# Gathers of the routing in a ring of eight rows, one gather per gate step, and splits and one-hots of the gate steps shared out anew

## The chip, the cores and the metric

The kernel runs on one core of one Trainium2 chip. The metric is the device time of one execution in microseconds (us), as the median of several runs. Engines: PE is TensorE's matmuls and PEld its weight loads, DVE is VectorE, ACT is ScalarE, POOL is GpSimd, SP is SyncE, which only issues DMAs here.

## The reference, cut to what matters

One residual block on 512 tokens of width 1024: a mixing layer (gated MLP and attention), then a layer of retrieved experts (PEER). The change lies in the second one:

```
q   = (xb @ w_query)                                   # 8 heads, two halves of 128
sc  = einsum('thpd,hpkd->thpk', q, sub_keys)           # 128 keys per half
s_top, i_top = top_k(sc, 16)
cand     = s_top[..., 0, :, None] + s_top[..., 1, None, :]
cand_idx = i_top[..., 0, :, None] * 128 + i_top[..., 1, None, :]
best, pos = top_k(cand, 16);  eidx = cand_idx at pos;  g = softmax(best)
h   = gelu(einsum('thkd,td->thk', expert_u[eidx], xb))
out = einsum('thk,thkd->td', g * h, expert_v[eidx])    # 16384 experts of width 1024
```

All is float32; the large matmuls are done as three float32r products of a high and a low part (hi, lo).

## The kernel before, in words

The 512 tokens are four tiles of 128. For tile 0 the experts are gathered row by row (128 gathers of u and 128 of v). For the other three tiles (384 tokens) every expert is multiplied densely: the first product gives expert_u times x for 128 blocks of 128 experts, Gelu follows, the result is multiplied by a gate matrix that is zero where an expert wasn't chosen, and the second product sums expert_v. Of the last tile, the last 64 tokens (UX) are an exception: their dot products with u are gathered early (two heads share a row block of 128 partitions, so there are 64 early gathers, HS), and the dense first product covers 320 columns only (NDU).

The stages after the mixing layer, in order of time:

1. The routing, a loop over heads h = 0 to 8. `candidates(h)` loads and splits a part of wq, multiplies, copies scores to SBUF (qt, scr) and takes the best keys on VectorE; `choose` works on the head before. Splits (`load_split`: DMA to raw, hi on ScalarE, lo on VectorE or GpSimd) are on GpSimd here. Two tiles of the first product go with each head, and 8 more (BRIDGE) stand in the last iteration. `indices_early` and `ready_early` put the indices of the early tokens together, `gather_early` gathers rows of u, `dots_early` multiplies them with xbu (in PSUM) and sums. The instructions of this stage are ordered by a scheduler with a cost model; a ring of four rows (ROWE) holds the gathered rows.
2. The gate steps, 48 of them (8 tokens each), in an order written out by hand for TensorE, VectorE, ScalarE and GpSimd (`manual_schedule`). A step makes two one-hot matrices: bm (compare on VectorE, times the gate on GpSimd) and am (compare on VectorE, or eight Abs and a Relu on ScalarE). Two steps later (LEAD) TensorE multiplies them (`products`), ScalarE copies the result to gst, and every second step a store of 1 MB goes to gd in DRAM. In between stand the rest of the early gathers and dots, and tiles of the first product: `here` says how many tiles are done by step n; the last six (LAST) come after the loop. For each tile of tokens `indices_of` and `gates_of` prepare indices and gates; those of the last tile need the early dots (`weights_early`).
3. The last stage, a loop over 64 chunks of two expert blocks. Every fourth chunk loads a group of gates (gc, 1.5 MB). `second_product` splits v, multiplies the activations (act) by the gates, splits them (wh, wl) and multiplies; the first product of the chunk 23 further on (AHEAD) follows. `route_gathered` does the routing of tile 0, two heads at a time, at every fourth chunk (ROUTE) from 0 to 12, and `gather_some` paces its gathers. Only TensorE's order is written out here.

Each engine works through its queue in order. The lines of the profile: L119 and L120 are hi and lo of a split, L484 the dot, L475 the early gather, L491 and L495 the index copies, L566 and L567 the positions in `pairs`, L689 to L692 the indices, L714 and L716 bm, L727, L728 and L730 am, L738 the gate products, L741 the copy to gst, L135 to L137 the first products, L901 to L905 the second, L884 to L891 act, wh and wl, L530 the Gelu.

## Time and profile before

| | |
|---|---|
| median of three runs | 1519.49 us (1512.56 to 1523.55) |
| the profiled execution's own time | 1515.91 us |
| span from its first to its last instruction | 1514.2 us |
| TensorE busy, mean granted clock | 1414.0 us (93%), 0.977 |
| VectorE, ScalarE, GpSimd busy | 1161.0 (77%), 631.6 (42%), 709.4 us (47%) |
| moved by DMA | 396.78 MB, mean 262 GB/s |

A matmul counts as busy from start to modelled end, so a busy TensorE at a lower granted clock does less. The shares are means over stages that differ: the mixing layer until about 240 us, the routing until 440, the gate steps until 644, then the last stage.

### The profile page before, as it was taken

What the parts mean: (1) busy time and instruction counts of PE and PEld (TensorE: products, weight loads), DVE (VectorE), ACT (ScalarE), POOL (GpSimd) and SP (SyncE); (2) the same over time, 40 slices, a digit from 0 to 9 for tenths busy, and PEclk for the clock granted to TensorE, in tenths of its full rate; (3) what the DMA queues carried; (4) which work ended last, traced back from release to release, by engine and by line L of the source; (5) the groups of instructions that cost most, each with busy time, mean ns of one, the idle gap of its engine ahead of it and who ended that gap; (6) DMA issues with size and microseconds to landing.
All of it is one profiled execution on the core that took longest, in us unless ns stands there. A gap on an engine that the chain in (4) does not pass through costs nothing.

```text
span 1514.2 us, 21710 instructions
## 1 busy us (share of the span) xinstructions
PE 1414.0 (93%) x7801; PEld 1243.9 (82%) x7801; DVE 1161.0 (77%) x2360; ACT 631.6 (42%) x1040; POOL 709.4 (47%) x465
## 2 busy tenths in 40 slices
PE   7999999989977876979999999999999999999998
PEld 6886678978977866878988888989898989888877
DVE  5437454879957769948898988887888888788883
ACT  5457543333336655533343433433433433333331
POOL 0000025566649997822445554555555554444530
PEclk9999999999989988989999999999999999999999
DMA  5352235366439998876888999999999999878892
GB/s 182 110 181 70 86 130 161 126 206 205 133 96 309 329 320 256 238 266 237 295 321 294 323 347 352 372 329 334 364 365 353 372 360 364 316 271 326 329 351 102
DMA packets 161100, 396.78 MB, mean 262 GB/s; under 512 B 11792, under 2 KB 74272, under 8 KB 158944
## 3 DMA queue, kind: packets, MB, share of 16 engines
q1 hardware_dynamic: 63696, 200.30, 37.3%
q0 software_dynamic: 46464, 168.61, 30.6%
q10 hardware_dynamic: 50832, 26.48, 6.1%
q8 instruction: 61, 1.00, 0.3%
q14 instruction: 47, 0.39, 0.1%
HBM read 363.86 MB, written 31.46 MB: 261 GB/s over the span
## 4 chain that ended last, share of the span: by engine, by line
PE 47%; DVE 20%; DMA 14%; issue 10%; POOL 7%; ACT 2%; SPq 0%; DVEq 0%; POOLq 0%; ACTq 0%
PE pu L135 6%; PE pu L137 6%; PE pu L136 6%; DMA row<-in_vd,eint 5%; PE pa L901 4%; PE pa L902 4%; PE pa L905 4%; DMA row<-in_ud,eint 3%; DMA rowe<-in_ud,eui 3%; PE pa L135 2%; PE pa L137 2%; PE pa L136 2%; DMA gc<-gd 2%; PE px L902 2%; PE px L905 2%
## 5 line engine op out<-in xcount | busy, mean ns | idle before, releaser
L119 ACT ACTIVATE hi<-raw 128x1024 fp32r<-128x1024 f32 x300 | 317.6, 1060 | 574.4 <-DMA raw<-in_vd 247.0
L120 DVE TENSOR_TENSOR lo<-raw,hi 128x1024 fp32r<-128x1024 f32 x240 | 292.5, 1220 | 85.0 <-ACT hi L119 84.0
L849 POOL DMA_INDIRECT row<-in_vd,eint x128 | 194.6, 1521 | 183.4 <-DVE acc L851 156.7
L838 POOL DMA_INDIRECT row<-in_ud,eint x128 | 188.6, 1474 | 187.5 <-DVE row L840 143.5
L137 PE MATMUL pu<-xch,lo 128*128 128x320 f32 x816 | 253.2, 310 | 12.1 <-POOL lo L120 7.7
L135 PE MATMUL pu<-xch,hi 128*128 128x320 f32 x816 | 254.9, 312 | 6.8 <-ACT act L530 6.8
L136 PE MATMUL pu<-xcl,hi 128*128 128x320 f32 x816 | 252.4, 309 | 0.0
L901 PE MATMUL pa<-hi,wh 128*128 128x512 f32 x512 | 200.6, 392 | 0.0
L902 PE MATMUL pa<-lo,wh 128*128 128x512 f32 x512 | 200.1, 391 | 0.0
L851 DVE SCALAR_TENSOR_TENSOR acc<-row,hw,acc 128x1024 f32<-128x1024 f32 x128 | 165.5, 1293 | 43.4 <-DMA row<-in_vd,eint 43.3
L120 POOL TENSOR_TENSOR lo<-raw,hi 128x1024 fp32r<-128x1024 f32 x60 | 144.3, 2413 | 98.1 <-ACT hi L119 97.6
L840 DVE SCALAR_TENSOR_TENSOR row<-row,xb 128x1024 f32<-128x1024 f32 x128 | 156.0, 1220 | 34.2 <-DMA row<-in_ud,eint 34.1
L137 PEld LDWEIGHTS pu<-xch,lo 128*128 128x128 f32 x816 | 154.3, 189 | 15.4 <-POOL lo L120 9.3
L135 PEld LDWEIGHTS pu<-xch,hi 128*128 128x128 f32 x816 | 154.6, 189 | 9.9 <-ACT act L530 8.3
L905 PE MATMUL pa<-hi,wl 128*128 128x512 f32 x512 | 157.7, 389 | 0.0
L136 PEld LDWEIGHTS pu<-xcl,hi 128*128 128x128 f32 x816 | 154.3, 189 | 1.6
L738 PE MATMUL pa<-bm,am 128*128 128x128 f32 x768 | 109.0, 302 | 35.9 <-POOL bm L716 32.1
L738 PEld LDWEIGHTS pa<-bm,am 128*128 128x128 f32 x768 | 101.6, 213 | 42.4 <-POOL bm L716 38.9
L901 PEld LDWEIGHTS pa<-hi,wh 128*128 128x128 f32 x512 | 96.7, 189 | 20.6
L902 PEld LDWEIGHTS pa<-lo,wh 128*128 128x128 f32 x512 | 96.6, 189 | 20.4
L905 PEld LDWEIGHTS pa<-hi,wl 128*128 128x128 f32 x512 | 96.3, 188 | 20.6
L902 PE MATMUL px<-lo,wh 128*128 128x512 f32 x256 | 101.6, 397 | 6.5 <-DVE lo L120 6.5
(212 smaller groups left out, 2612.6 us busy)
## 6 DMA issues: line engine op xcount, KB each, us to landing
raw<-in_uT SPq DMA_DIRECT2D x128, 512.0 KB, 6.1
raw<-in_vd SPq DMA_DIRECT2D x128, 512.0 KB, 5.8
gd<-gst ACTq DMA_DIRECT2D x24, 1024.0 KB, 6.7
gc<-gd SPq DMA_DIRECT2D x16, 1536.0 KB, 9.9
raw<-in_w_in SPq DMA_DIRECT2D x20, 512.0 KB, 4.6
raw<-in_wq SPq DMA_DIRECT2D x16, 512.0 KB, 3.7
raw<-in_w_out SPq DMA_DIRECT2D x8, 512.0 KB, 4.2
bt<-in_bias SPq DMA_DIRECT2D x8, 256.0 KB, 7.5
```

Of the source, the lines that this page charges most:

```text
L119: nc.scalar.activation(hi, raw, AF.Copy)
L120: eng.tensor_tensor(lo, raw, hi.bitcast(F32), op=ALU.subtract)
L135: nc.tensor.matmul(ps, lh[0], rh[0], start=first, stop=False)
L136: nc.tensor.matmul(ps, lh[0], rh[1], start=False, stop=False)
L137: nc.tensor.matmul(ps, lh[1], rh[0], start=False, stop=last)
L738: nc.tensor.matmul(ps[:, i * P:(i + 1) * P], am[:, 4 * q + i, :], bm[:, 4 * q + i, :], start=True, stop=True)
L838: nc.gpsimd.indirect_dma_start(out=row, out_offset=None, in_=ud, in_offset=bass.IndirectOffsetOnAxis(ap=eint[:, j:j + 1], axis=0))
L849: nc.gpsimd.indirect_dma_start(out=row, out_offset=None, in_=vd, in_offset=bass.IndirectOffsetOnAxis(ap=eint[:, j:j + 1], axis=0))
L851: nc.vector.scalar_tensor_tensor(acc0, row, hw[:, j:j + 1], acc0, op0=ALU.mult, op1=ALU.add)
L901: nc.tensor.matmul(accs[t][half], wh[:, b, tok], w[b][0][:, ds_], start=first, stop=False)
L902: nc.tensor.matmul(accs[t][half], wh[:, b, tok], w[b][1][:, ds_], start=False, stop=False)
L905: nc.tensor.matmul(accs[t][half], wl[:, b, tok], w[b][0][:, ds_], start=False, stop=last)
```

## The change

Early gathers: six instead of three are issued in each routing iteration, from a ring of eight rows (ROWA) in the routing's own pool rq; their dots follow one iteration later, and all that were issued are finished before that pool closes. The 28 that remain go one per step, in steps 0 to 27, with a ring of four in the gate steps' pool gp; dots follow three steps later (LAGE). The early weights are formed at steps 33 and 35, and the gates of the last tile are made a second time at step 39, for its last 64 tokens.

Copies: the index copies of the early tokens, the positions in `pairs` (for `route_gathered` too) and the casts of `indices_of` go from VectorE to ScalarE.

Gate steps: the last two of eight columns of each first one-hot are made on ScalarE, six on VectorE. Two tiles of the first product come at step 0, the other twelve are spread over all steps. Splits alternate between GpSimd and VectorE, and after the loop all are on VectorE. The first chunk's v is loaded and split before the last two tiles.

Last stage: xb0, acc0, the first sc and the first gc are loaded by GpSimd's queue; each later gc is loaded a group ahead. `route_gathered` comes at chunks 0, 6, 12 and 18.

```diff
+ROWA = 8
-LAGE = 2
+LAGE = 3
-SLOW = 20
-EARLY = 3
+EARLY = 6
-SOON = 25
+ON_ACT = 2
-ROUTE = 4
+ROUTE = 6
...
-        row = gat.tile([P, D], F32, name="rowe", tag="rowe", bufs=ROWE)
+        routing = ExitStack()
+        rq = routing.enter_context(tc.tile_pool(name="rq", bufs=1))
+        row = rq.tile([P, D], F32, name="rowe", tag="rowe", bufs=ROWA)
...
-        def gather_early(n):
-
-            rows = []
+        def gather_early(n, rows_of, n_rows):
+
             for j in early[:n]:
-                row = gat.tile([P, D], F32, name="rowe", tag="rowe", bufs=ROWE)
+                row = rows_of.tile([P, D], F32, name="rowe", tag="rowe", bufs=n_rows)
...
-                rows.append((j, row))
+                issued.append((j, row))
             del early[:n]
-            issued.append(rows)
...
-            nc.vector.tensor_copy(eu[P - UX:P, js], eidx[P - UX:P, TT - 1, h * TOPK:(h + 1) * TOPK])
+            nc.scalar.copy(eu[P - UX:P, js], eidx[P - UX:P, TT - 1, h * TOPK:(h + 1) * TOPK])
...
-            nc.vector.tensor_copy(eui[:, js], eu[:, js])
+            nc.scalar.copy(eui[:, js], eu[:, js])
...
-            nc.vector.tensor_scalar(top[:, 1, :, 0, :], pos[:, :, 0, :], float(NK), None, op0=ALU.mult)
-            nc.vector.tensor_copy(top[:, 1, :, 1, :], pos[:, :, 1, :])
+            nc.scalar.activation(top[:, 1, :, 0, :], pos[:, :, 0, :], AF.Copy, scale=float(NK))
+            nc.scalar.copy(top[:, 1, :, 1, :], pos[:, :, 1, :])
...
-            dots_early(1)
-            gather_early(EARLY)
+            dots_early(0)
+            gather_early(EARLY, rq, ROWA)
...
         ready_early(NH - 2)
+        dots_early(0)
         routing.close()
...
-            nc.vector.tensor_copy(ei, eidx[:, t, :])
+            nc.scalar.copy(ei, eidx[:, t, :])
...
-            nc.vector.tensor_copy(ff, ii)
+            nc.scalar.copy(ff, ii)
...
-        def first_one_hot(g, c, on_act):
+        def first_one_hot(g, c):
             it, ni, gt = g
-            ts_ = slice(c * TC, (c + 1) * TC)
-            full = [P, TC, P]
+            ts_ = slice(c * TC, (c + 1) * TC - ON_ACT)
+            full = [P, TC - ON_ACT, P]
             am = gp.tile([P, TC, P], F32, name="am", tag="am", bufs=LEAD + 1)
...
+            nc.vector.tensor_tensor(am[:, 0:TC - ON_ACT, :], iota_k[:, None, :].to_broadcast(full),
+                                    it[:, 0, ts_, None].to_broadcast(full), op=ALU.is_equal)
+
+            for i in range(TC - ON_ACT, TC):
+                nc.scalar.activation(am[:, i, :], iota_k, AF.Abs, bias=ni[:, c * TC + i:c * TC + i + 1])
+            rest = am[:, TC - ON_ACT:, :]
+            nc.scalar.activation(rest, rest, AF.Relu, scale=-1.0, bias=1.0)
             return am
...
+        def rows_of_v(c):
+
+            return [load_split(vd.rearrange("(a b) d -> a b d", b=NB)[:, c * BC + b, :]) for b in range(BC)]
+
...
-        def split_next():
+        def split_next(eng=nc.gpsimd):
             nonlocal split
             if split < AHEAD * BC:
-                split_tile(split, nc.gpsimd)
+                split_tile(split, eng)
                 split += 1
...
+        own = steps - UX // TC
...
-                    ams[n] = first_one_hot(gs[t], c, n % 2 == 1 and n < SOON)
+                    ams[n] = first_one_hot(gs[t], c)
+                if n < own - 7:
+                    gather_early(1, gp, ROWE)
                 dots_early(LAGE)
-                if n < steps:
-                    gather_early((len(early) + max(0, SOON - n) - 1) // max(1, SOON - n))
...
+                if n == own - 7:
+                    assert not early
+                    dots_early(0)
+                    weights_early(0)
+                if n == own - 5:
+                    weights_early(1)
+                if n == own - 1:
+
+                    gs[t] = gates_of(GT + t, ff.pop(t))
+                here = LEAD + (AHEAD * BC - i0 - LAST * BC - LEAD) * (n + 1) // steps
                 while split - len(ready) - i0 < min(here, AHEAD * BC - i0 - LAST * BC):
                     multiply_tile()
-                    split_next()
+                    split_next(nc.vector if split % 2 else nc.gpsimd)
             while ready:
+                if split == AHEAD * BC and not weights:
+                    weights[0] = rows_of_v(0)
                 multiply_tile()
-                split_next()
+                split_next(nc.vector)
...
-        nc.sync.dma_start(xb0, xbd[0])
+        nc.gpsimd.dma_start(xb0, xbd[0])
...
-        nc.sync.dma_start(acc0, x2d[0])
+        nc.gpsimd.dma_start(acc0, x2d[0])
...
+        def load_gates(q, eng):
+            gcs[q] = ep.tile([P, NG, GB, TG], F32, name="gc", tag="gc", bufs=2)
+            eng.dma_start(gcs[q].rearrange("p n b t -> p (n b t)"), gd[q].rearrange("p n f -> p (n f)"))
+
         def second_product(c):
-            if (c * BC) % GB == 0:
...
+            w = weights.pop(c) if c in weights else rows_of_v(c)
+            if c == 0:
+                load_gates(0, nc.gpsimd)
+            gc = gcs[c * BC // GB]
...
+            if c == 1:
+                with tc.issue_after(loads[-1]):
+                    load_gates(1, nc.sync)
+            elif c * BC % GB == 0 and 0 < c * BC < NB - GB:
+                load_gates(c * BC // GB + 1, nc.sync)
```

## Rows read from the trace of the kernel before

**Rows 1.** Busy time by stretch: length, PE, PEld, DVE, ACT, POOL (instructions), PE clock, DMA share, GB/s.

```profile
310.00:440.00 130.00, 116.44 (x668) 107.58 (x666) 113.03 (x488) 40.68 (x69) 77.89 (x44) 0.95 0.50 162
...
644.00:680.00 36.00, 27.70 (x145) 24.81 (x144) 15.56 (x25) 12.97 (x19) 9.58 (x4) 0.86 0.74 264
...
800.00:900.00 100.00, 93.88 (x489) 82.66 (x488) 88.48 (x163) 35.97 (x51) 52.38 (x37) 0.97 0.89 325
900.00:1300.00 400.00, 399.42 (x2204) 361.31 (x2204) 342.00 (x436) 153.88 (x218) 213.89 (x144) 1.00 0.96 356
...
450.00:580.00 130.00, 100.43 (x668) 96.64 (x667) 95.01 (x127) 77.65 (x165) 117.54 (x81) 0.89 0.96 319
```

**Rows 2.** Order of time on GpSimd, one gate step: start, duration, instruction, idle before.

```profile
473.22 1.90 POOL L716 TENSOR_TENSOR bm<-bm,gt 128x1024 f32<-128x1024 f32 x1
475.27 0.98 POOL L475 DMA_INDIRECT rowe<-in_ud,eui  x1 [0.16 <-issue]
...
477.52 2.39 POOL L120 TENSOR_TENSOR lo<-raw,hi 128x1024 fp32r<-128x1024 f32 x1
479.86 1.90 POOL L716 TENSOR_TENSOR bm<-bm,gt 128x1024 f32<-128x1024 f32 x1
```

**Rows 3.** Order of time on TensorE: a late gate step, then four tiles' first and last matmul.

```profile
637.45 2.05 PE L738 MATMUL pa<-bm,am 128*128 128x128 f32 x16 [0.21 <-POOL bm L716]
...
643.83 0.39 PE L135 MATMUL pu<-xch,hi 128*128 128x320 f32 x1
...
657.86 0.31 PE L137 MATMUL pu<-xch,lo 128*128 128x320 f32 x1
```

**Rows 4.** Groups of instructions on VectorE, 240 to 432 us: busy, mean ns, idle before.

```profile
L484 DVE SCALAR_TENSOR_TENSOR rowe<-rowe,px 128x1024 f32<-128x1024 f32 x12 | 14.5, 1213 | 7.9 <-DMA rowe<-in_ud,eui 7.8
L495 DVE CAST eui<-eu 128x16 int32<-128x16 f32 x4 | 11.1, 2779 | 2.0 <-DMA eu<-eidx 2.0
L491 DVE COPY eu<-eidx 64x16 f32<-64x16 f32 x4 | 8.8, 2206 | 0.1
...
L566 DVE TENSOR_SCALAR top<-pos 128x48 f32<-128x48 uint32 x8 | 6.0, 752 | 0.0
```

**Rows 5.** Order of time on VectorE, a step with one gather, and the next.

```profile
579.83 1.22 DVE L714 TENSOR_TENSOR bm<-iota_k,pa 128x1024 f32<-128x1024 f32 x1
...
583.24 1.22 DVE L714 TENSOR_TENSOR bm<-iota_k,pa 128x1024 f32<-128x1024 f32 x1
```

**Rows 6.** Groups of instructions on ScalarE, 440 to 645 us.

```profile
L741 ACT COPY gst<-pa 128x512 f32<-128x512 f32 x96 | 55.3, 585 | 78.0 <-PE pa L738 69.9 <-DMA gd<-gst 7.9
L727 ACT ACTIVATE am<-iota_k,ni 128x128 f32<-128x128 f32 x96 | 29.3, 389 | 1.8 <-ACT gst L741 1.8
...
L728 ACT ACTIVATE am<-am 128x1024 f32<-128x1024 f32 x12 | 12.7, 1058 | 0.4
```

**Rows 7.** DMA issues of the page: queue, count, KB each, us to landing.

```profile
raw<-in_uT SPq DMA_DIRECT2D x128, 512.0 KB, 6.1
...
gd<-gst ACTq DMA_DIRECT2D x24, 1024.0 KB, 6.7
```

**Rows 8.** Order of time on VectorE, where the gate steps begin.

```profile
439.58 0.23 DVE L689 CAST ei<-eidx 128x128 int32<-128x128 f32 x1 [10.81 <-PE pu L137]
...
441.79 1.22 DVE L714 TENSOR_TENSOR bm<-iota_k,pa 128x1024 f32<-128x1024 f32 x1 [1.26 <-ACT ni L705]
```

**Rows 9.** Order of time on VectorE, the second norm.

```profile
210.55 1.28 DVE L156 SCALAR_TENSOR_TENSOR xs<-x,rstd,g2row 128x1024 f32<-128x1024 f32 x1
...
219.11 3.21 DVE L156 SCALAR_TENSOR_TENSOR xs<-x,rstd,g2row 128x1024 f32<-128x1024 f32 x1
```

**Rows 10.** Waits of TensorE, 240 to 440 us: total, times, longest.

```profile
PE pu L135 <- ACT act L530: 7.6, 1, 7.6
```

**Rows 11.** Order of time on TensorE, after the gate steps.

```profile
663.61 0.64 PE L135 MATMUL pu<-xch,hi 128*128 128x320 f32 x1 [5.44 <-ACT act L530]
...
669.33 0.80 PE L902 MATMUL px<-lo,wh 128*128 128x512 f32 x1 [2.86 <-DVE lo L120]
```

**Rows 12.** Waits from 640 us to the end.

```profile
DVE act L884 <- DMA gc<-gd: 30.3, 8, 16.2
```

41 lines of the change are left out of this document (10 added, 31 removed).

## The prediction

> **What bounds the kernel now.** I read the busy time by stage first [rows 1]. From 900 to 1300 us TensorE is busy 399.42 of 400 us at full clock: the last stage, from about 680 us on, runs at TensorE's own rate, so whatever lets it start earlier moves the end by as much. Before it there are losses. From 450 to 580 us, in the gate steps, TensorE is busy 100.43 of 130 us at a granted clock of 0.89, while GpSimd is busy 117.54 and the DMA engines 0.96 of the time. From 644 to 680 us, where the last stage begins, TensorE has 27.70 of 36 us at 0.86. From 310 to 440 us, in the routing, VectorE has 113.03 of 130 and TensorE 116.44.
>
> Then GpSimd's order of time in the gate steps [rows 2]. One step with a tile to split goes from 473.22 to 479.86, 6.64 us: the product bm 1.90, two gathers of about 0.96 with 0.3 us between them, the split lo 2.39, and the next product at once. GpSimd waits for nobody there, so it sets the pace, with the DMA engines close behind. TensorE needs far less in a step: 16 matmuls for the gates take 2.05 us [rows 3]. Four tiles of the first product took 643.83 to about 658.0, so 3.5 us a tile [rows 3].
>
> Now the 14 tiles of the loop all fall into the first 18 steps (20 tiles over 25 steps, stopped at 14), on top of up to two gathers a step. Later steps have neither, and TensorE just follows at 2.05 us with 0.21 us of waiting.
>
> **The gate steps.** The early gathers are 64. Before, the routing had done 12 of the dot products [rows 4] and 52 were left for the gate steps. After, six are issued in each of iterations 3 to 8 of the routing loop (16 new ones come in at 3, 5 and 7, so six are always there): 36 in the routing, 28 left, one per step in steps 0 to 27. The tiles are spread: two at step 0, 12 over 48 steps, a quarter of a tile per step. Half of those splits go to VectorE. Two of eight columns of each first one-hot go to ScalarE, where before every second one-hot of steps 1 to 23 did so whole.
>
> The nearest rows to a step after the change are in this trace: from 579.83 to 583.24 VectorE does both one-hots whole and one dot product, 3.41 us, with one gather on GpSimd [rows 5]. The parts of a step with a gather, after:
> VectorE: bm and dot 1.14 each (the 3.41 is three operations of one length), am three quarters of it, 0.85, an eighth of a split at 1.14 = 0.14: 3.27 us.
> GpSimd: 1.90 + 0.98 + 0.16 between them + an eighth of 2.39 = 3.34.
> ScalarE: two copies at 0.585 [rows 6], two Abs at 29.3/96 = 0.305, a Relu of 256 columns between 0.305 and a quarter of 1.058, so 0.3, a quarter of a tile's hi and Gelu (taken as 1.5 us): 2.5.
> TensorE: 2.05 + 3.5/4 = 2.9.
> DMA: half a store of 1024 KB [rows 7], one gather of 128 rows of 4 KB, a quarter of a 512 KB tile: 1.18 MB. At the 319 GB/s of 450 to 580 us [rows 1] that is 3.7 us.
> Transfers lead by little, so a step takes 3.8 us, one end being the 3.41 of rows 5, the other the 4.6 that two gathers and a product fill on GpSimd without a tile (1.90 + 2 x 1.28 + 0.16). A step without a gather is TensorE's 2.9, and I take 3.0.
>
> The sum: the first bm starts at 441.8 as now [rows 8]; 28 x 3.8 = 106 and 19 x 3.0 = 57 bring the last bm to 605, and the last product, two steps behind, to 613. Now it ends at 644. I take 28 us of these 31, since a tile's 3.5 us will at times fall where gate products are due. The ends: 28 x 3.41 + 19 x 2.9 gives a gain of 44, 28 x 4.6 with 19 x 3.3 a gain of 3.
>
> One row speaks against splits on VectorE beside GpSimd. VectorE's norm step with two SBUF inputs took 1.28 us at 210.55 and 3.21 us at 219.11, when GpSimd had begun a split [rows 9]: 1.9 us more. A VectorE split in the loop then costs 3.0 instead of 1.14, an eighth of 1.9 = 0.24 per step: VectorE 3.5, still under the 3.8, so the sum stays, but three resources then stand within 0.3 us of each other, and I give the rival of a slower pace more for it. The Trainium skill (SBUF — State Buffer, Who interferes with whom) states that a VectorE instruction with two SBUF inputs and a GpSimd instruction that reads SBUF share a port by an exclusive lock. By that rule the dot products, whose one input is in PSUM, are free of it and the splits are not; rows 5 and 9 agree. By it GpSimd's step rises too, by an eighth of 1.14, to 3.5, and the sum stays as it is.
>
> **The routing.** VectorE gains 24 dot products there: at 1.14 to 1.21 us, 27 to 29 us. It loses the eui casts 11.1, the eu copies 8.8 and the scaling of positions 6.0, 25.9 us [rows 4]; the small cast beside it is left out. These are long for 16 to 48 columns (2779 ns for 16), so they are mostly waiting, and on ScalarE each should take some 0.3, as its 128-column Abs does [rows 6]. The net is +1 to +3 on VectorE. Its cover: VectorE waits 10.81 us for TensorE's bridge tiles before the gate steps begin at 439.58 [rows 8]; the last six dots (7 us) fall into that. GpSimd gets 24 gathers at 1.28, 31 us, onto 77.89 of 130 busy [rows 1]: it fits. Four of six must wait until dots free their rows in the ring of eight, with the wq splits queued behind on GpSimd and TensorE behind those. ScalarE gets copies that wait for VectorE and for the eu transfer, and hi, qt, scr and act queue behind them. I take +3 us. The ends: -8, if the 7.6 us for which TensorE waits for act behind the softmax [rows 10] go away; +17, if the 25.9 us are not given back and 28 less the 11 of cover remain.
>
> **The start of the last stage.** After 644 TensorE still has six tiles, 21 us. It does four, then waits 5.44 us for act and 2.86 for a split [rows 11], at a granted clock of 0.86 over the 36 us [rows 1]: 8.3 us idle plus up to 5 at the lower clock. The act stands behind ScalarE's wh, and that behind the first gate load: VectorE waits 16.2 us for gc [rows 12]. After: the tail's splits are on an idle VectorE (1.14, not 2.39), the first weights are loaded during the tail, and gc, xb0, acc0 and the first sc go by GpSimd's queue, idle then, so nothing stands ahead of the tiles on SP's. VectorE's 16.2 us for gc begin before the last gate product ends, so the gates are there within 16 us of it; product, wh and wl for 640 columns add an estimated 3 (from 1024 columns in 1.06 us on ScalarE and 1.14 on VectorE), 19 in all, and 21 us of tiles cover them. I take -9; the ends are 0 and -13.
>
> **The last stage.** gc is now loaded a group ahead. Of the 30.3 us that VectorE waited for it, 14.1 are in seven later waits [rows 12]. TensorE has cover for most: from 680 on it loses mainly in 800 to 900, 6.1 us idle and the clock at 0.97 [rows 1]. Routing of gathered heads at chunks 0, 6, 12, 18 instead of 0, 4, 8, 12 thins VectorE's load there. Heads 2 and 3 are first asked for at gather 48, chunk 11, after chunk 6, so this delays nothing. I take -4, from -10 to +4. Gates of the last half tile computed twice: three transposes, about 1 us beside other work, nothing.
>
> **The sum.** +3 - 28 - 9 - 4 = -38 us. Against the profiled execution's own 1515.9 (span 1514.2) that is 1478; the median of the runs is 3.6 us higher. I predict 1478. A measurement here tells about 1% from no change, so faster means under 1504 and slower over 1535.
>
> **Rivals.** First, a slower pace: transfers, VectorE and GpSimd so close that in-order waits make a gathering step 4.2 and the others 3.3. The last product then ends near 630, a gain of 14, and the total is 1492. For it speaks the DMA share of 0.96 now and the two-input row; against it, rows 5, where such a step runs at 3.41. Chance 0.15. Second, the routing pays: the moved casts were not waste, or the six gathers per head do not get done in time and, as the ring's pool must be empty before the gate steps' tiles can take its space, hold up those. +17 instead of +3: 1492. VectorE's 113 of 130 speak for it, the 10.81 of cover against. 0.12. Third, slower than before: ScalarE's in-order queue in the routing. Some 24 moved copies now wait there for VectorE or for the eu transfer. One such wait, the exponent of the softmax, cost TensorE 7.6 us. The gain without routing is 41, so it decides from six of these upwards; one in each of eight heads is 61 us and gives 1536. Against it: TensorE waited for act just once in that stretch [rows 10], and two PSUM tiles and five split tiles stand between. 0.07. Fourth, good ends together, gate steps at 3.41 and nothing lost at the start: +3 - 44 - 13 - 4 = -58, 1458. 0.08. The forecast itself keeps 0.55, from 1464 to 1494; 0.03 is for what I don't see.
>
> The range 1456 to 1505 leaves out most of the third rival and the tails of the others. Faster by over 1%: 0.55 + 0.08 and three quarters of the first two rivals, 0.83; within 1%: 0.10; slower: 0.07.
>
> **What would show it.** Gate steps about 3.8 us apart with one gather and about 3.0 without, last gate product near 613 us on the old clock, gate-step GpSimd no longer without gaps; 36 dots ahead of the first bm; VectorE's routing busy time within 5 us of now; TensorE without the 5.44 us gap after the last gate product; gc waits nearly gone. Wrong: bm steps over 4.2 us, a first bm later than 450, ScalarE copies of top, eu or eui with idle time ahead of them and TensorE waiting for act or lo behind.

## The result and the profile after

The changed kernel takes 1506.96 us (median of 10 runs, 1499.53 to 1508.44) beside 1517.79 of the kernel before in the same session: a ratio of 0.9924, 95% interval 0.9904 to 0.9944. The 1478 of the prediction and its range, 1456 to 1505, are missed; the sign of the whole is right. The profiled execution has a span of 1506.3 us, 7.9 less than before; at 1508.44 us it is the slowest of the ten.

I split this at two places that each trace shows as a row: the first bm on VectorE and the end of the last gate product on TensorE. Order of time of the kernel after, on VectorE, then TensorE:

```profile
454.32 1.22 DVE L717 TENSOR_TENSOR bm<-iota_k,pa 128x1024 f32<-128x1024 f32 x1 [1.76 <-ACT ni L708]
...
464.64 1.95 PE L740 MATMUL pa<-bm,am 128*128 128x128 f32 x16
...
631.49 3.73 PE L740 MATMUL pa<-bm,am 128*128 128x128 f32 x32
```

The same two of products in the kernel before:

```profile
447.15 2.97 PE L738 MATMUL pa<-bm,am 128*128 128x128 f32 x16 [2.48 <-POOL bm L716]
...
641.13 2.94 PE L738 MATMUL pa<-bm,am 128*128 128x128 f32 x24 [0.26 <-DVE am L730]
```

The first bm comes at 454.32 where it came at 441.79 [rows 8]: **the routing costs 12.5 us**, forecast 3. From there to the end of the last product it was 641.13 + 2.94 - 441.79 = 202.3 us and is 631.49 + 3.73 - 454.32 = 180.9: **the gate steps gain 21.4**, forecast 28. From the last product to the end of the span it was 870.1 and is 871.1: **the last stage loses 1.0** where 9 + 4 were forecast as gains. 12.5 - 21.4 + 1.0 = -7.9.

Busy time by stretch, kernel after (columns as in rows 1):

```profile
310.00:440.00 130.00, 110.41 (x609) 100.39 (x608) 122.17 (x504) 42.04 (x80) 92.99 (x63) 0.92 0.71 243
...
634.00:670.00 36.00, 33.32 (x198) 31.15 (x198) 22.57 (x55) 16.44 (x26) 2.36 (x4) 0.95 0.84 297
...
760.00:780.00 20.00, 14.42 (x75) 13.14 (x74) 11.60 (x31) 4.05 (x6) 6.60 (x4) 0.83 0.62 239
...
740.00:900.00 160.00, 143.70 (x758) 126.44 (x758) 134.75 (x265) 59.21 (x86) 73.24 (x51) 0.97 0.84 306
900.00:1300.00 400.00, 399.14 (x2197) 360.68 (x2196) 343.47 (x441) 152.62 (x217) 211.41 (x144) 1.00 0.95 356
```

and the stretch of the kernel before that rows 1 do not have:

```profile
740.00:900.00 160.00, 151.96 (x798) 133.71 (x797) 145.25 (x300) 58.04 (x83) 82.73 (x56) 0.98 0.88 319
```

Against [rows 1], TensorE has lost 6.0 us in the routing and won 5.6 where the last stage begins (33.32 of 36, before 27.70). Between 740 and 900 it has lost 8.3. From 900 on it is full, as before. So what the start of the last stage won was given back by 900 us.

**Where the routing stalls.** One chain, read backwards from TensorE's wait. Order of time on VectorE, ScalarE and TensorE, kernel after:

```profile
313.32 1.22 DVE L488 SCALAR_TENSOR_TENSOR rowe<-rowe,px 128x1024 f32<-128x1024 f32 x1 [8.22 <-DMA rowe<-in_ud,eui]
...
321.87 0.24 ACT L568 ACTIVATE top<-pos 128x48 f32<-128x48 uint32 x1 [9.27 <-DVE rep L553]
...
323.43 0.64 PE L138 MATMUL pu<-xbh,hi 128*128 128x320 f32 x1 [7.71 <-ACT act L534]
```

The dots of the first batch stand in VectorE's queue ahead of the key search, and wait 8.22 us for the gathered rows. The search is late by that; ScalarE's copy of the positions waits for it 9.27 us with hi and act behind; TensorE waits 7.71 us for act. It looks like the third rival, the copies on ScalarE. The experiments say otherwise: the copy is where the wait is shown, not what makes it.

**The gate steps** run at VectorE's own rate where nothing else is due: two bm stand 3.14 us apart with one dot between them, where the forecast had 3.27 for VectorE. Order of time on VectorE, kernel after:

```profile
461.13 4.23 DVE L123 TENSOR_TENSOR lo<-raw,hi 128x1024 fp32r<-128x1024 f32 x1 [4.72 <-ACT hi L122]
...
493.32 1.21 DVE L717 TENSOR_TENSOR bm<-iota_k,pa 128x1024 f32<-128x1024 f32 x1
494.46 0.94 DVE L727 TENSOR_TENSOR am<-iota_k,pa 128x768 f32<-128x768 f32 x1
495.32 1.21 DVE L488 SCALAR_TENSOR_TENSOR rowe<-rowe,px 128x1024 f32<-128x1024 f32 x1
...
496.46 1.21 DVE L717 TENSOR_TENSOR bm<-iota_k,pa 128x1024 f32<-128x1024 f32 x1
...
578.82 1.23 DVE L123 TENSOR_TENSOR lo<-raw,hi 128x1024 fp32r<-128x1024 f32 x1 [7.00 <-ACT hi L122]
```

The new wait is in the rows of lo: VectorE's queue stands still until ScalarE has made hi, with every later bm and am behind it. The first lo also took 4.23 us beside GpSimd's split, where the one at 578.82 took 1.23.

**The start of the last stage.** VectorE waits 2.84 us for the first gate load, before 16.20 [rows 12], and TensorE's longest gap is 2.68, before 5.44 [rows 11]. Order of time on VectorE, then TensorE, kernel after:

```profile
651.30 0.89 DVE L896 TENSOR_TENSOR act<-act,gc 128x320 f32<-128x320 f32 x2 [2.84 <-DMA gc<-gd]
...
653.74 0.66 PE L918 MATMUL px<-hi,wh 128*128 128x512 f32 x1 [2.68 <-ACT wh L897]
```

### The profile page after: what moved, and what is told of

It reads as the page before. It is cut to its first block, busy times and chain, and to the rows that moved or that the text cites. A ratio compares the mean times of both kernels' runs of the same rounds, so it can differ in the third digit from the quotient of the medians.

```text
span 1506.3 us, 21702 instructions
## 1 busy us (share of the span) xinstructions
PE 1410.9 (94%) x7804; PEld 1241.8 (82%) x7804; DVE 1151.1 (76%) x2345; ACT 645.4 (43%) x1116; POOL 682.8 (45%) x458
## 4 chain that ended last, share of the span: by engine, by line
PE 35%; DVE 23%; DMA 19%; issue 13%; POOL 7%; ACT 3%; ACTq 0%; DVEq 0%; SPq 0%; POOLq 0%
DMA row<-in_vd,eint 7%; DMA row<-in_ud,eint 6%; PE pu L138 4%; PE pu L140 4%; PE pu L139 4%; DVE lo L123 4%; PE pa L138 3%; PE pa L139 3%; PE pa L140 3%; DVE rowe L488 3%; DVE row L851 2%; PE pa L918 2%; PE pa L919 2%; PE pa L922 2%; POOL row L860 2%
## 5 line engine op out<-in xcount | busy, mean ns | idle before, releaser
L123 DVE TENSOR_TENSOR lo<-raw,hi 128x1024 fp32r<-128x1024 f32 x251 | 311.4, 1242 | 114.1 <-ACT hi L122 113.2
L860 POOL DMA_INDIRECT row<-in_vd,eint x128 | 201.6, 1575 | 194.7 <-DVE acc L862 159.9
L849 POOL DMA_INDIRECT row<-in_ud,eint x128 | 177.0, 1383 | 201.7 <-DVE row L851 157.4
L123 POOL TENSOR_TENSOR lo<-raw,hi 128x1024 fp32r<-128x1024 f32 x49 | 118.6, 2434 | 79.3 <-ACT hi L122 79.0
L740 PE MATMUL pa<-bm,am 128*128 128x128 f32 x768 | 100.5, 289 | 27.5 <-POOL bm L719 14.5
L740 PEld LDWEIGHTS pa<-bm,am 128*128 128x128 f32 x768 | 94.7, 201 | 32.8 <-POOL bm L719 26.8
L919 PEld LDWEIGHTS pa<-lo,wh 128*128 128x128 f32 x512 | 96.7, 189 | 20.4
```

Of the source, the lines that this page charges most:

```text
L123: eng.tensor_tensor(lo, raw, hi.bitcast(F32), op=ALU.subtract)
L740: nc.tensor.matmul(ps[:, i * P:(i + 1) * P], am[:, 4 * q + i, :], bm[:, 4 * q + i, :], start=True, stop=True)
L849: nc.gpsimd.indirect_dma_start(out=row, out_offset=None, in_=ud, in_offset=bass.IndirectOffsetOnAxis(ap=eint[:, j:j + 1], axis=0))
L860: nc.gpsimd.indirect_dma_start(out=row, out_offset=None, in_=vd, in_offset=bass.IndirectOffsetOnAxis(ap=eint[:, j:j + 1], axis=0))
L919: nc.tensor.matmul(accs[t][half], wh[:, b, tok], w[b][1][:, ds_], start=False, stop=False)
```

## The experiments

Verdicts are ratios to the kernel before, run beside each kernel; edits are to the kernel after unless the text says otherwise. "First product" and "loop" are the first matmul of L740 and the time from it to the end of the last one: 464.64 and 170.6 us after, 447.15 and 196.9 before. Stages are read from one profile per kernel, and their scatter can be told from kernels that share a stage: the routing of after stands unchanged in e4, e5, e6, e10, e13, e16 and e17, and their first bm, with that of after, lies between 452.95 and 457.79. The last stage of after stands unchanged in e5, e6, e7 and e11, and TensorE's busy time in 740 to 900 us lies between 143.70 (after, the lowest) and 149.98. Differences between kernels run at different times are given in medians and judged by the intervals of their ratios.

### First set: is it the copies on ScalarE?

**e1_pairs_dve**, the two copies of pairs back on VectorE:

```
-nc.scalar.activation(top[:, 1, :, 0, :], pos[:, :, 0, :], AF.Copy, scale=float(NK))
-nc.scalar.copy(top[:, 1, :, 1, :], pos[:, :, 1, :])
+nc.vector.tensor_scalar(top[:, 1, :, 0, :], pos[:, :, 0, :], float(NK), None, op0=ALU.mult)
+nc.vector.tensor_copy(top[:, 1, :, 1, :], pos[:, :, 1, :])
```

> The two copies of pairs (positions times 128, and second positions) go back from ScalarE to VectorE in the routing and in the gathered tokens' routing of the last stage; all else as after. Main theory (ScalarE's in-order queue holds copies that wait for VectorE, 20 us of such waits in the routing and 20 in the last stage, and what stands behind them is late): the first bm comes 4 to 6 us before the 454.3 us of after, the ten lost microseconds between chunks 6 and 8 come back in part, and the time is 1494 to 1500. Rival A (the loss is VectorE's sixteen more dots in the routing and the later load order in the last stage): first bm within 2 us of 454, chunk 8 within 2 us of 796 us, time 1505 to 1510. Rival B (the copies were well moved): VectorE's 128x48 casts cost the routing 6 us more, 1512.

1507.92 us, 0.9938 [0.9913, 0.9963]. First bm 459.69, later than 454.32; TensorE has 147.48 us in 740 to 900.

**e2_copies_dve**, eu, eui, ei and ff too:

```
-nc.scalar.copy(eu[P - UX:P, js], ...)   # likewise eui, ei, ff
+nc.vector.tensor_copy(eu[P - UX:P, js], ...)
```

> All five moved small copies (the two of pairs, eu, eui, ei and ff) go back to VectorE. Main theory: what the run before gives and some 3 us more in the routing, because eu's copy on ScalarE waited 13.9 us for VectorE's eidx in three waits: first bm at 446 to 449, 1491 to 1498. Rival A: within 2 us of after, 1505 to 1510, the 36 dots bound the routing. Rival B (VectorE's casts of eu and eui at 2.2 and 2.8 us each beside the gathers come back): first bm at 460 or later, 1512 to 1516.

1510.96 us, 0.9968 [0.9943, 0.9992]. First bm 462.38. Both first bm lie past those of all eight profiles with the copies on ScalarE, so the routing is slower, not faster: **my theory of the copies falls** for the routing.

**e3_early3**, three early gathers per head:

```
-EARLY = 6
+EARLY = 3
+SOON = 25
-                    gather_early(1, gp, ROWE)
+                    gather_early((len(early) + max(0, SOON - n) - 1) // max(1, SOON - n), gp, ROWE)
```

> Three early gathers per head instead of six, the rest at up to two per gate step in steps 0 to 24, as the kernel before had them; the ring of eight rows, the copies on ScalarE and all else as after. Main theory (copies on ScalarE delay the routing): first bm at most 5 us earlier than 454.3, and the gate steps 0 to 24 take back more than that, time 1508 to 1515. Rival A (the dots themselves delay the routing): the 16 to 18 dots that leave the routing are 18 x 1.2 = 21 us of VectorE; first bm 10 us or more earlier, at 441 to 445; the gate steps then take 10 to 20 us longer, time 1503 to 1515.

1535.33 us, 1.0114 [1.0074, 1.0153]: slower than the kernel before, and outside both forecasts. First bm 447.42, 6.9 earlier, so the dots do cost the routing. The loop took 208.1 us, 37.5 longer: 18 more gathers at 2.1 us each, where I had expected 10 to 20 us.

**e4_route4**, the gathered routing at chunks 0, 4, 8 and 12:

```
-ROUTE = 6
+ROUTE = 4
```

> The gathered tokens' routing in the last stage stands at chunks 0, 4, 8 and 12 again instead of 0, 6, 12 and 18; all else as after. Main theory (the copies on ScalarE and not the place of this routing make the loss between chunks 6 and 8): the stall moves to chunk 4 or 8 and stays some 8 us, time 1504 to 1509. Rival (the spacing of six meets the gate load at chunk 4 to 8 badly): chunk 8 starts 8 to 10 us earlier, at 786 to 788 us, and the time is 1496 to 1499.

1503.35 us, 0.9918 [0.9892, 0.9943], TensorE 148.78 us in 740 to 900, so part of the loss is still there. Neither number came: the time is just under the main theory's 1504 to 1509 and far from the rival's 1496 to 1499. The interval does not tell it from after.

### Second set: where the gate steps' gain is from

**e5_split_pool**, the splits inside the steps all on GpSimd:

```
-                    split_next(nc.vector if split % 2 else nc.gpsimd)
+                    split_next(nc.gpsimd)
```

> Inside the gate steps every split of a uT tile goes to GpSimd, as in the kernel before; behind the steps (the tail) the splits stay on VectorE; all else as after. Theory now (the copies on ScalarE are not the loss; the gate steps gain 27 us, and the sixteen gathers that left them at 2.1 us each are more than all of it, so the other edits of the steps cost some 7): VectorE no longer waits for ScalarE's hi (26.2 us in six waits of after), GpSimd has 2.4 us more per second tile; the loop between first and last gate product takes 163 to 170 us (after 170.3) and the time is 1500 to 1507. Rival (the splits on VectorE are a gain, GpSimd bounds a step with its product of bm, a gather and a split): the loop takes 176 to 185 us, time 1513 to 1522.

1510.33 us, 0.9945 [0.9924, 0.9967]; loop 170.7. No difference in the loop, so the rival (176 to 185) is out; the theory's 163 to 170 is just missed, as is its time. Waits of VectorE from 440 to 640 us (total, times, longest), after and in this run:

```profile
DVE lo L123 <- ACT hi L122: 26.2, 6, 7.0
DVE bm L717 <- PE pa L740: 9.2, 5, 3.7
```

```profile
DVE bm L717 <- PE pa L740: 22.6, 11, 6.9
DVE rowe L488 <- DMA rowe<-in_ud,eui: 14.2, 11, 1.8
DVE lo L123 <- ACT hi L122: 10.9, 2, 10.5
```

The wait for hi goes down by 15.3 us and the waits for TensorE and for the gathered rows (4.1 us after) come up by 23.5: it was cover, not a bound.

**e6_am_alternate**, the first one-hot whole on one engine, as before:

```
-                    ams[n] = first_one_hot(gs[t], c)
+                    ams[n] = first_one_hot(gs[t], c, n % 2 == 1 and n < SOON)   # body as before
```

> The first one-hot am is built whole on VectorE in even steps and whole on ScalarE in odd steps up to step 24, as in the kernel before, in place of six columns on VectorE and two on ScalarE in every step; all else as after. Theory (the other edits of the steps cost some 7 us, and the split one-hot is one of them, since each step then needs both engines): the loop takes 165 to 171 us, time 1502 to 1508. Rival (the split one-hot is the gain): a step without help from ScalarE has 1.2 us of am on VectorE instead of 0.95, over 48 steps and with the uneven steps 6 to 15 us more: loop 176 to 185 us, time 1513 to 1522.

1507.5 us, 0.993 [0.9906, 0.9955]; loop 176.2. Splitting the one-hot is worth 5.6 us of the loop; the total does not show it.

**e7_gathers_behind**, each head's early dots and gathers behind its products:

```
-            dots_early(0)
-            gather_early(EARLY, rq, ROWA)
             if h < NH:
                 cands.append(candidates(h))
...
+            dots_early(0)
+            gather_early(EARLY, rq, ROWA)
             if h > 0:
```

> In the routing, each head's early dots and gathers are put behind that head's scores and first products instead of ahead of them; same number of gathers, copies on ScalarE, all else as after. Theory (what the routing lost is the batch of gathers itself: ten gathers back to back on GpSimd, 12.3 us from 307.65, stand ahead of the splits that TensorE needs, and VectorE waits 8.2 us for the first of them with the position search behind it): the stall of 7.7 us at head 4 goes, the first bm comes 5 to 10 us before 454.3, time 1498 to 1503. Rival (36 dots of 1.2 us are simply too much for VectorE, wherever they stand): first bm within 3 us of 454, time 1504 to 1510.

1502.31 us, 0.9895 [0.9863, 0.9928]; first bm 451.04, first product 461.61: 3 us of the 12.5. e12, e15 and e18 share this routing and have their first bm at 451.70, 451.13 and 449.13, so the gain is more than scatter.

**e8_gathers_only**, the kernel before with the gathers alone:

```
-EARLY = 3
+EARLY = 6
+ROWA = 8
-            dots_early(1)
-            gather_early(EARLY)
+            dots_early(0)
+            gather_early(EARLY, rq, ROWA)
```

> The kernel before with one part of the change alone: six early gathers per head in the ring of eight rows with their dots in the next head, the other 28 over the gate steps 0 to 24. Copies on VectorE, splits on GpSimd, am alternating, tiles early, load order and ROUTE all as before. Theory (moving sixteen gathers out of the steps saves 2.1 us each there and costs 11 to 13 in the routing; the other edits of the steps cost 7): first bm 453 to 456, loop 161 to 168 us against 196.6 before, time 1492 to 1500, faster than after. Rival A (the other edits of the steps are gains as forecast): loop 175 to 185 us, time 1508 to 1514. Rival B (with the copies on VectorE the routing pays more, as in the run with all copies on VectorE): first bm 460 or later, time 1500 to 1508.

1509.21 us, 0.9956 [0.9933, 0.998]. First bm 455.85, loop 173.0. **The gathers alone give 23.9 of the loop's 26.3 us and cost 14.1 in the routing.** The start of the last stage is as before (27.74 of 36 us in 634 to 670). From the first bm to the end of the last product e8 takes 178.4 us, before 202.3, after 180.9 (177.5 to 182.1 in the kernels that share after's steps): by this measure, which was the forecast's, the other edits of the steps together bring nothing that shows.

### Third set: dots or gathers, and how far to go

**e9_no_dots**: the 36 dots of the routing are left out, the gathers stay.

```
-            dots_early(0)
+            dots_early(0, True)      # takes them off the list, issues nothing
```

> As after, but the 36 dots of the routing are left out (the gathers stay), so part of the gathered tokens' gate weights is missing; the work of the gate steps is the same. Theory A (VectorE's dots, and its wait for the first gathered row with the position search behind it, are what the routing lost): the last eidx, at 447.1 us in after, comes at 425 to 430, and the first gate product, at 464.4, at 444 to 448. Theory B (the gathers themselves, 0.95 us each on GpSimd ahead of the splits, are it): the last eidx moves by the last batch of dots alone, to 440 or later, and the first gate product comes at 457 or later.

1494.37 us, one run. The last eidx comes at 426.64 (447.34 after), the first bm at 441.88 (after 454.32), the first product at 452.19, where theory A had 444 to 448. Before, the first bm stood at 441.79: **without the 36 dots, and the 8.5 us for which they wait for rows, the 12.5 us are gone, though all 36 gathers are still there.** Groups on VectorE from 240 to 460 us, this run, then the two that answer to them after:

```profile
L592 DVE TENSOR_TENSOR pa<-bpos,bits 128x288 uint32<-128x288 uint32 x8 | 15.6, 1955 | 0.7
L579 DVE TENSOR_TENSOR cand<-top 128x96 f32<-128x96 f32 x8 | 13.8, 1725 | 8.2 <-ACT top L572 8.2
```

```profile
L488 DVE SCALAR_TENSOR_TENSOR rowe<-rowe,px 128x1024 f32<-128x1024 f32 x36 | 43.4, 1215 | 8.5 <-DMA rowe<-in_ud,eui 8.5
L589 DVE TENSOR_TENSOR pa<-bpos,bits 128x288 uint32<-128x288 uint32 x8 | 8.5, 1062 | 0.2
L576 DVE TENSOR_TENSOR cand<-top 128x96 f32<-128x96 f32 x8 | 7.8, 969 | 0.3 <-ACT top L569 0.3
L576 DVE TENSOR_TENSOR cand<-top 128x48 f32<-128x48 f32 x16 | 7.6, 473 | 0.0
```

43.4 us of dots are gone, and yet up to its last eidx VectorE is busy only 25.9 us less (145.73, after 171.68): the mask and the 96-column candidates, the same instructions on the same data, grew by 7.1 and 6.0.

**e11_early8**, eight per head:

```
-EARLY = 6
+EARLY = 8
```

> Eight early gathers per head instead of six, so 48 in the routing and 16 in the gate steps; all else as after. Theory (a gather costs some 0.8 us in the routing, 12.5 us for 16 of them, and 2.1 us in a gate step): twelve more out of the steps: loop 143 to 150 us against 170.3, first gate product 8 to 14 us later than 464.4, time 1490 to 1498. Rival A (the ring of eight is then full, and GpSimd waits for VectorE's dots with the splits behind it): first gate product 20 us or more later, time 1504 to 1515. Rival B (without a gather a step is bound by GpSimd, PE or the waits for hi and not by VectorE): loop 158 to 166 us, time 1505 to 1512.

1510.81 us, 0.9961 [0.9939, 0.9983]. First product 477.01, 12.4 later; loop 159.9, 10.7 less: rival B. Between six and eight, one more gather costs in the routing (1.0 us) about what it saves in a step (0.9).

### Fourth set: the last stage

**e10_last_as_before**: ROUTE = 4, the last stage's pairs on VectorE, each gate load at its own chunk.

```
-ROUTE = 6
+ROUTE = 4
+            if n == ND: ...     # pairs: ScalarE in the routing, VectorE in the last stage
-            if c == 1:
-                with tc.issue_after(loads[-1]):
-                    load_gates(1, nc.sync)
-            elif c * BC % GB == 0 and 0 < c * BC < NB - GB:
-                load_gates(c * BC // GB + 1, nc.sync)
+            if c and (c * BC) % GB == 0:          # ahead of the rows of chunk c
+                load_gates(c * BC // GB, nc.sync)
```

> Everything behind the first chunk as in the kernel before: the copies of pairs on VectorE in the last stage (on ScalarE still in the routing), the gathered routing at chunks 0, 4, 8 and 12, each gate load at the start of its own chunk; the early load of chunk 0's rows and GpSimd's queue for the first loads stay. Theory (these three together are the loss of the last stage): from chunk 2 to chunk 8 94 to 97 us against 103.2 in after and 94.6 in before, time 1497 to 1502. Rival (the loss is in the state in which the stage starts, as the earlier start of chunk 0 shifts the loads against the routing): 100 to 104 us, time 1503 to 1508.

1496.85 us, 0.9863 [0.9847, 0.988]: faster than both kernels, the intervals of this and of after do not meet. TensorE 153.10 us in 740 to 900.

**e12_behind_route4**: ROUTE = 4, the last stage's pairs on VectorE, the gathers behind as in e7; the gate loads as after.

```
-ROUTE = 6
+ROUTE = 4
+            if n == ND: ...     # pairs as in e10
```

> After with three edits together: early dots and gathers behind each head's scores and products, the gathered routing at chunks 0, 4, 8 and 12, and its copies of pairs on VectorE in the last stage. Theory (each edit pays by itself: 2 to 5, 2 to 4 and 3 to 5 us): first gate product at 461, chunk 2 to chunk 8 in 95 to 98 us, time 1495 to 1500, faster than both kernels. Rival (the edits of the last stage overlap, and the profile of each differs by as much without an edit): time 1500 to 1505.

1501.97 us, 0.9897 [0.988, 0.9913]; 146.33 us in 740 to 900. With the gate loads as after the loss stays.

**e13_gc_start**: that edit alone.

```
-                    load_gates(1, nc.sync)
...
+                load_gates(c * BC // GB, nc.sync)     # the last six lines of e10's diff
```

> As after, with one edit: from chunk 1 on each gate load is issued at the start of the chunk that first uses it, as in the kernel before, and not a block of four chunks ahead; copies on ScalarE and routing at chunks 0, 6, 12 and 18 as after. Theory (the gate loads a block ahead are the loss of the last stage, since the run with ROUTE 4 and VectorE's copies but with these loads ahead still took 103.1 us from chunk 2 to chunk 8): 94 to 98 us there, time 1497 to 1502. Rival (all three edits of the last stage are needed, or none matters by itself): 100 to 104 us, time 1503 to 1508.

1505.34 us, 0.9933 [0.991, 0.9956]. In 740 to 900 TensorE has all of it back, 155.72 us, and yet the total is not told from after's. It lost at the start: from 630 to 700 TensorE is busy 59.23 us at a clock of 0.90, after 65.98 at 0.98, and waits for act 10.8 us in two waits.

**e14_before_prefetch**: the kernel before with the gate loads of after from chunk 1 on.

```
-            if (c * BC) % GB == 0:
-                gc = ep.tile([P, NG, GB, TG], F32, name="gc", tag="gc", bufs=2)
...
+            elif c * BC % GB == 0 and 0 < c * BC < NB - GB:
+                load_gates(c * BC // GB + 1, nc.sync)
```

> The kernel before with one edit: from chunk 1 on each gate load is issued a block of four chunks ahead, as in after. Theory (the loads ahead cost 8 us): chunk 2 to chunk 8 takes 100 to 104 us against 94.6, time 1522 to 1528, slower than before. Rival A (the loads ahead gain, as forecast: 16.2 us of wait at chunk 4 and 30.3 in all go): chunk 2 to 8 in 88 to 92, time 1512 to 1515. Rival B: within 2 us of before.

1523.75 us, 1.0048 [1.0025, 1.007]: slower, as its theory had it. From 644 to 680 TensorE wins 5.4 us (33.13, before 27.70), from 740 to 900 it loses 5.3 (146.63), and then 3.5 more from 900 to 1000 (96.46 of 100).

**e15_last_and_behind**: e10 with the gathers behind, the edit of e7.

```
+            dots_early(0)                      # both lines behind the head's products
+            gather_early(EARLY, rq, ROWA)
```

> The last stage behind its first chunk as before (copies of pairs on VectorE, routing at chunks 0, 4, 8 and 12, each gate load at its own chunk), and in the routing the early dots and gathers behind each head's products. Theory (both edits keep their gains): first gate product at 461 to 462, chunk 2 to chunk 8 in 95 to 97 us, time 1492 to 1496, the fastest. Rival (the gain of the gathers behind was the scatter between runs): 1496 to 1499, as with the last stage alone.

1494.62 us, 0.9857 [0.9824, 0.9889], the fastest. Its profiled execution took 1505.36, the other four 1493.95 to 1494.86, so I do not read its stages. Whether it beats e10, the intervals do not tell.

**e16_gc_route4**: e10 with the copies of pairs left on ScalarE.

```
-            if n == ND: ...     # that line of e10 taken out: ScalarE in both stages
```

> As after, with each gate load at its own chunk and the gathered routing at chunks 0, 4, 8 and 12; the copies of pairs stay on ScalarE. It differs from the run with the whole last stage as before (1496.85) in those copies alone. Theory (the place of the routing and the gate loads together are the loss, the copies cost nothing by themselves): 1495 to 1499. Rival (the copies on ScalarE, which wait there for VectorE, are part of it): 1500 to 1504.

1502.57 us, 0.9911 [0.9884, 0.9938], 5.7 more than e10; the intervals just miss each other. In the last stage, then, the copies on ScalarE seem to cost: from 640 to 900 us ScalarE waits 18.1 us for VectorE's positions, longest 9.1, and in 630 to 700 TensorE waits 13.3 us for act (e10 7.0). This profile reaches the stage 5.1 us later than e10's; counted over 60 us from each one's last gate product, TensorE has 50.14 us against 52.95.

**e17_first_gate_ahead**: e10, but the second gate load behind the rows of chunk 1 as after, only the later ones at their own chunk.

```
+            if c == 1:
+                with tc.issue_after(loads[-1]):
+                    load_gates(1, nc.sync)
-            if c and (c * BC) % GB == 0:
+            if c * BC > GB and (c * BC) % GB == 0:
```

> As the run with the last stage as before (1496.85), except that the second gate load keeps its place of after, behind the rows of chunk 1; the third and later ones are at the start of their own chunk. Theory (the loads ahead are a gain for the second gate load, which otherwise goes out at the hand-over ahead of the tiles, 62.95 us of TensorE in 630 to 700 against 65.98, and a loss for the later ones, 143.70 in 740 to 900 against 153.10): 65 to 66 us in 630 to 700 and 152 to 156 us in 740 to 900 both, time 1491 to 1496. Rival (the two cannot be had together, as the second gate load moves the loads behind it): 740 to 900 at 144 to 149 us again, time 1497 to 1503.

1507.37 us, 0.9935 [0.9913, 0.9957]: 10.5 worse than e10, with intervals apart, by the place of **one** load. The rival's mechanism held, and the time is worse than its 1497 to 1503. Busy time by stretch, e17, then e10:

```profile
630.00:700.00 70.00, 66.34 (x384) 60.72 (x383) 48.95 (x148) 31.85 (x46) 9.92 (x10) 0.98 0.78 272
740.00:900.00 160.00, 143.84 (x758) 126.38 (x757) 142.14 (x283) 58.57 (x83) 78.86 (x54) 0.97 0.87 312
```

```profile
630.00:700.00 70.00, 62.95 (x353) 57.96 (x353) 51.11 (x173) 28.78 (x40) 11.01 (x11) 0.95 0.69 243
740.00:900.00 160.00, 153.10 (x832) 135.97 (x832) 146.27 (x282) 61.80 (x87) 87.69 (x57) 1.00 0.92 337
```

**e18_first_ahead_behind**: e17 with the gathers behind.

```
+            dots_early(0)                      # as in e7
+            gather_early(EARLY, rq, ROWA)
```

> The kernel of the run before with the early dots and gathers of the routing behind each head's products. Theory (2 us from the routing as in the earlier runs): 1489 to 1494, the fastest. Rival (no effect that can be told): within 2 us of the run before.

1502.51 us, 0.99 [0.9863, 0.9937]: neither forecast came. It is 7.9 more than e15, though the intervals overlap, and equal to e12, from which it differs in the later gate loads only: the planner issues the third at 681.52 in e12 and at 680.20 in e18, wherever the program asks for it.

Order of time on SP's queue, e17, then e10: the second and third gate load (gc), and the third load of the gathered routing's scores (sc), of four.

```profile
656.34 0.33 SPq L887 DMA_DIRECT2D gc<-gd  x1
...
684.72 0.38 SPq L887 DMA_DIRECT2D gc<-gd  x1
...
697.31 0.43 SPq L837 DMA_DIRECT2D sc<-s0d  x1
```

```profile
636.68 0.33 SPq L887 DMA_DIRECT2D gc<-gd  x1
...
682.15 0.38 SPq L837 DMA_DIRECT2D sc<-s0d  x1
...
694.71 0.38 SPq L887 DMA_DIRECT2D gc<-gd  x1
```

The second load goes out 20 us later in e17 and lets the tiles through: TensorE has 3.4 us more in 630 to 700. The third, whose line in the program is the same in both, goes out 10 us earlier, now ahead of the scores, and between 740 and 900 TensorE has 9.3 us less.

## Why the prediction missed

**The routing, +3 forecast, +12.5 measured: the step that failed first.** I had 24 dots at 27 to 29 us, 25.9 us given back by the moved copies, so +1 to +3 on VectorE, and 11 us of cover. The dots were right: 28.9 us more. The cover was there in the main: VectorE's last eidx comes 22.1 us later, the first bm 12.5. What failed is the 25.9 us given back. Busy time from 240 us to the end of the last eidx, before and after (columns as in rows 1):

```profile
240.00:425.46 185.46, 172.36 (x979) 157.05 (x978) 158.32 (x747) 65.94 (x109) 112.79 (x62) 0.97 0.48 156
```

```profile
240.00:447.57 207.57, 187.33 (x1048) 170.35 (x1047) 171.68 (x772) 70.36 (x133) 131.26 (x82) 0.95 0.58 196
```

VectorE is busy 13.4 us more, where +1 to +3 was forecast, and idle 8.8 us more.

The 25.9 us were "mostly waiting", as I wrote, and I did not ask for what. The trace of the kernel before has it. Order of time, two of the same casts on VectorE, then GpSimd beside the second:

```profile
303.90 0.15 DVE L495 CAST eui<-eu 128x16 int32<-128x16 f32 x1
...
395.81 7.06 DVE L495 CAST eui<-eu 128x16 int32<-128x16 f32 x1
...
395.74 7.10 POOL L120 TENSOR_TENSOR lo<-raw,hi 128x1024 fp32r<-128x1024 f32 x3
```

The second cast ends with GpSimd's three splits. So it is with all 16 copies of [rows 4]: four had no split or copy on GpSimd beside them and took 0.15 to 0.19 us; each of the other twelve took 0.53 to 7.06 us and ended within 0.07 us of the end of a split on GpSimd. GpSimd makes the same 35 splits in that stretch after (83.8 and 83.4 us), so another instruction of VectorE meets them. Of the 25.9 us, 11.4 came back: 1.3 in the mask (7.2 us before, 8.5 after) and 10.1 in the two longest forms of the candidates, which went from

```profile
L574 DVE TENSOR_TENSOR cand<-top 128x48 f32<-128x48 f32 x16 | 3.1, 195 | 0.0
L574 DVE TENSOR_TENSOR cand<-top 128x96 f32<-128x96 f32 x8 | 2.2, 277 | 0.0
```

in the kernel before to 7.6 and 7.8 after. For the first bm the move is worth less still: putting the copies back (e2) makes it 8.1 us later, and e8, which never moved them, has it 1.5 us later than after, inside the scatter. The end of +17, with nothing given back, was nearer than +3. e9 shows that the delay goes with the dots.

**The rival of ScalarE's queue** was right that such waits would appear (20.4 and 19.7 us for the two copies of pairs, in the routing) and wrong that they set the time there: e1 and e2 take them away and the routing gets slower. In the last stage it seems right, by e16 for 5.7 us.

**The gate steps, -28 forecast, -21.4 measured.** The sum had 28 steps with a gather at 3.8 us, 19 without at 3.0, and 8 us from the last bm to the end of the last product. Order of time on VectorE, after, the bm of step 28 and of the last step:

```profile
560.00 1.21 DVE L717 TENSOR_TENSOR bm<-iota_k,pa 128x1024 f32<-128x1024 f32 x1
...
624.83 1.22 DVE L717 TENSOR_TENSOR bm<-iota_k,pa 128x1024 f32<-128x1024 f32 x1 [0.71 <-PE pa L740]
```

The 28 steps took 105.7 us, 3.77 each. That this is the forecast's 3.8 is partly luck: the first step alone took 11.0 us and the other 27 took 3.5 each. The 19 steps without a gather took 64.8 us, 3.41 each, against 57, and the end 10.4 against 8: this is the term that failed. TensorE is busy 54.72 us in the 19 steps, 2.9 a step as in the sum; what the sum put at 0.1 a step is its waiting, 11.4 us from 560 us to the end, for am and bm, while VectorE waits 16.1 us for hi and 7.2 for TensorE. In e5, without splits on VectorE inside the steps, the same 19 steps take 62.7 us, so those splits are not the cause; it stays open.

The long first step: from the first bm to the first product it was 5.4 us and is 10.3. TensorE's queue has the two tiles of step 0 ahead of the first product and works on them from 454.01 to 464.64 with one wait. Order of time on TensorE, after:

```profile
456.52 0.63 PE L140 MATMUL pu<-xch,lo 128*128 128x320 f32 x1 [1.95 <-POOL lo L123]
```

Before, one tile stood there, to 444.7, and 2.48 us of waiting for bm. That is read from the traces and was not tested.

From the first product on, 23.9 us are the gathers that moved (e8), 5.6 the split one-hot (e6), nothing the splits on VectorE (e5); these do not add up, and no run takes the rest apart. The rival of a slower pace, 4.2 us with a gather, did not come. The price of a gather in a step is not one number: 2.1 us when two fall into a step (e3), 0.9 between 28 and 16 of them in 48 steps (e11).

The first lo on VectorE took 4.23 us while GpSimd split a tile at 461.87, and the one at 578.82, when GpSimd was idle, took 1.23. The trace so agrees with the rule of the Trainium skill (SBUF — State Buffer, Who interferes with whom) that a VectorE instruction with two SBUF inputs contends with a GpSimd instruction that reads SBUF. It changed nothing in the loop here, since e5 takes these splits away and the loop stays.

**The start of the last stage, -9 forecast,** came nearly as forecast by itself: 5.6 us more of TensorE in 36, at a clock of 0.95 for 0.86, together some 8 us of work at full clock (an estimate from these four numbers).

**The last stage, -4 forecast, turned out a loss of about 8** (8.3 us of TensorE in 740 to 900, where kernels that share the stage differ by up to 6). Two steps failed. First, "14.1 us in seven later waits" for gc had nothing to give. Waits of VectorE from 1300 us to the end, before and after:

```profile
DVE act L884 <- DMA gc<-gd: 12.9, 4, 4.6
```

```profile
DVE act L896 <- DMA gc<-gd: 12.7, 4, 4.1
```

They lie where TensorE is full, and are still there. I had counted a wait without looking when it falls. Second, the place of the second gate load was counted as a gain alone, "so nothing stands ahead of the tiles" on SP's queue; what it does to the loads behind it was put at nothing. The kernel before had its first two gate loads together at 650.67, the second one far ahead of its use. The change moves that one behind the rows of chunk 1, which lets the tiles through at the start, and more is lost between 740 and 900. e17 against e10 puts the whole at 10.5 us, and e14 against the kernel before at 7.9, where the later loads are a group ahead too; both are clear of noise. e18 against e15 has 7.9, with overlapping intervals. In e13 the same step back shows no gain on the total: TensorE loses 6.8 us in 630 to 700. That the copies on ScalarE are why is argued from e16, not tested by itself.

The largest gap of that loss is the same in after and in e17. Order of time on TensorE, then on VectorE, after:

```profile
769.97 0.64 PE L140 MATMUL pu<-xch,lo 128*128 128x320 f32 x1 [5.58 <-DVE lo L123]
...
764.75 0.29 DVE L551 MAX8 top<-sc 128x8 f32<-128x128 f32 x1 [4.91 <-DMA sc<-s0d]
```

and in e17:

```profile
770.11 0.64 PE L138 MATMUL pu<-xch,hi 128*128 128x320 f32 x1 [5.75 <-ACT act L534]
...
764.91 0.29 DVE L551 MAX8 top<-sc 128x8 f32<-128x128 f32 x1 [4.30 <-DMA sc<-s0d]
```

In both, VectorE's queue stands for the last load of scores, and the next search and the split behind it are late; in e17 ScalarE waits 7.26 us for that search with act behind. This load leaves SP's queue at 757.33 and 757.75, in e10 at 744.45, where VectorE does not wait for it. The load of scores before it went out behind the third gate load in after (700.48 and 687.63) and e17, ahead of it in e10. e4, e12 and e18 have the order and the wait of e17 (4.4, 3.6 and 3.6 us), e13, e15 and e16 the order of e10 and no such wait after 740 us. From 760 to 780 TensorE has 14.25 us in e17 and 19.21 in e10, and the clock is 0.83 in after and e17: about half of the 9.3 us. **What stays open** is the other half, why the planner orders the loads so, and e14, which has no such wait and still loses; no run moves the load of scores by itself.

On the profiled executions the sum of the three misses is 9.5 + 6.6 + 14.0 = 30.1 us, and 38 forecast less 7.9 found is the same.

## What to carry to other kernels

A short instruction with a long duration can be a wait in disguise: look for what ends together with it on another engine. If that stays, moving the instruction away frees little more than its own work, so price it by its shortest instance, and expect the next instruction to inherit the wait. Before counting a wait as a gain, look at when it falls and whether the engine that sets the end is idle then. Where a planner orders the queues, one load moved for a gain at one place can cost more at the next; give each edit its own run, since here 10 us hung on the place of one load.

## What the runs showed of the hardware that I had not expected

The same vector instructions took very different times as other work around them came and went: the 128x96 candidates in the mean 277 ns before, 969 after and 1725 with the dots left out; the 16-column cast of eui 2779 ns before and 1122 in e2, and single ones 0.15 and 7.06 us. The long ones among the copies of before ended with a split on GpSimd, to within 0.07 us. The five copies, in the mean 0.18 to 2.8 us on VectorE, took 0.20 to 0.24 (pairs, eu, eui) and 0.30 to 0.40 (ei, ff) on ScalarE.
